# Hybrid token mixer and mixture-of-experts trunk on one core: an adaLN row's sum over the partitions placed in the middle of the following tile

## Chip, core and metric

The kernel runs on one core of a Trainium2 chip. The metric is device microseconds of one execution; three runs of the kernel before gave 3958.64, 3955.86 and 3944.15 us, the median is 3955.86 us. Profiles come from one execution each. PE is TensorE, DVE is VectorE, ACT is ScalarE, POOL is GpSimd, SP is SyncE; PEq, SPq and so on are the queues from which these engines take their instructions in order.

## What is computed

One layer on 4096 tokens of width 1024. A conditioning vector `c` gives six rows of 1024 numbers (shift, scale and gate for each of two sub-layers), which modulate a normalised `x`; the first sub-layer projects that into four head groups and mixes tokens, the second is a mixture of 64 experts.

```python
c_act = jax.nn.silu(c)
mod = c_act @ ada_w[l] + ada_b[l]                      # 1024 -> 6 x 1024
sh_m, sc_m, gt_m, sh_f, sc_f, gt_f = jnp.split(mod, 6, axis=-1)
h = modulate(rmsnorm(x, mix_norm_g[l]), sh_m, sc_m)
p = h @ w_in[l]                                        # split into the head groups
o_a, o_b, o_c, o_d = ...                               # delta rule, spatial gating, short conv, RWKV-7
x = x + gt_m[:, None, :] * (jnp.concatenate([o_a, o_b, o_c, o_d], -1) @ w_out[l])
h = modulate(rmsnorm(x, ffn_norm_g[l]), sh_f, sc_f)
x = x + gt_f[:, None, :] * hier_moe(h, ...)
return rmsnorm(x, final_norm_g)
```

The change concerns how four of the six rows of `mod` (numbers 2 to 5) are made. Rows 0 and 1 are needed for the first tile and are made before it.

## The kernel before

`run` goes through the stages `first`, `gdn`, `rwkv`, `outp`, `moe` and `final`. Only `first` is touched. It works on eight tiles (t = 0 to 7) of 512 tokens. For tile t, `first_tile` (line 930) has PE project the normalised and modulated tokens `h` with several slices of `w_in`: four matmul groups for the value half of the spatial gate and eight small columns (lines 944 to 958, the "sv" part), two groups for the other half (960 to 965, "su"), then after a reciprocal square root (966) and `norm()` (967) two groups for the low-rank inputs (974 to 981, "lx"). Tiles 0, 1 and 2 also do a short convolution (1002); tiles 3 to 7 do not. The spatial gating's own matmuls (1014) end the tile.

While a tile is projected, the input of the next is prepared. `h_rows` (255) loads its four blocks of 128 rows of `x` through the SP queue into the buffer ring with the tag `hx`, which has six buffers, and sums the squares on ACT. `h_norm` (270), called by `norm()` in the middle of `first_tile`, scales the rows on DVE. `h_make` (276) transposes them on PE (282), modulates on ACT, splits into a high and a low part on DVE (286, 288) and stores both to DRAM through the POOL queue (289, 290); its eight steps are woven between the matmuls of the second lx group (tiles 3 to 6) or of the convolution (tiles 0 to 2). The buffers of the x rows come free when the last transpose has read them, at the end of the tile.

The rows of `mod` ride along. A row is a sum over 1024 = 8 x 128 inputs: `ada_step` (199) loads one block of `ada_w`, 128 x 1024, through the SP queue into the same `hx` ring (208) and adds it, times the conditioning vector, to an accumulator on DVE (211, 213). The accumulators have the tag `adaa`, with two buffers. After eight steps `ada_row` (215) loads a row of `ada_b` through SP (219), sums the accumulator over the partitions with two fp32 matmuls against a column of ones (223, two instructions each on PE), adds the halves to the bias on DVE (224) and stores the row to DRAM through SP (227, 230), where stages much later read it. The 32 steps are dealt out five per tile (1129), so rows 2, 3, 4 and 5 end in tiles 1, 3, 4 and 6, the steps that end them being the third, first, fourth and second of their tile.

What sets the order: within `first` the order of PE's instructions is that of the program text (`manual_schedule(engines=PE)`, 1122). The order on the other engines and their queues is worked out by a planner from its own estimates of time, with program order as the priority; every engine then takes its instructions strictly in that order, each waiting for its inputs and for a free buffer. PE's order at a tile with a finished row is therefore: the row's four matmul instructions, then the tile's sv, su and lx parts.

When `first` is over its buffers are given to `gdn`, whose weights are loaded (351, tile `hraw`) into memory that the `hx` ring and others held.

Of the kernel before, what the change touches and what calls it, by code (L numbers as in the profile page):

```python
# [8 lines left out]
F32 = mybir.dt.float32  # L9
# [10 lines left out]
D = 1024  # L20
# [14 lines left out]
def tp(tc, name, bufs=1, **k):  # L35
    return tc.tile_pool(name=name, bufs=bufs, reuse_waits="tile", **k)
# [6 lines left out]
class Trunk:  # L43
# [168 lines left out]
            else:  # L212
                V.scalar_tensor_tensor(acc, w, self.cact[:, k:k + 1], acc, op0=ALU.mult, op1=ALU.add)

    def ada_row(self, pool, psum, j, ptag):

        nc, A = self.nc, self.A
        row = pool.tile([128, D], F32, name="adar", tag="adaa", bufs=2)
        nc.sync.dma_start(row[0:1], A["ada_b"][0:1, j * D:j * D + D])
        for n in range(2):  # L220
            s = slice(n * 512, n * 512 + 512)
            ps = psum.tile([128, 512], F32, name="adap", tag=ptag)
            nc.tensor.matmul(ps[0:1], self.one_c, self.ada_acc[:, s], start=True, stop=True)
            nc.vector.tensor_tensor(row[0:1, s], row[0:1, s], ps[0:1], op=ALU.add)
        if j == 3:

            nc.sync.dma_start(self.modd[j:j + 1].rearrange("o (k q) -> o q k", k=KT),
                              row[0:1].rearrange("o (q k) -> o q k", k=KT))
        else:
            nc.sync.dma_start(self.modd[j:j + 1], row[0:1])  # L230
# [859 lines left out]
    def first(self):  # L1090
        tc, A = self.tc, self.A
        with ExitStack() as c:
            pool_ = lambda n, b=1, **k: Pool(c.enter_context(tp(tc, n, b, **k)), n, b)
            wp, hp, pool, hw = pool_("f_w"), pool_("f_h", 18), pool_("f"), pool_("f_hw")
            psum = BufPsum(pool_("f_ps", space=PSUM), {"big": 6, "ada": 2})
            raw = lambda: hw.tile([128, D], F32, name="wraw", tag="hx", bufs=6)
            self.ada_begin(hw, psum, "ada")
            xs, ss = self.h_rows(hw, 0)
            self.h_norm(hw, xs, ss)
            self.f_sv = [wp.tile([128, KT, 264], F32R, name=f"sv{x}") for x in ("h", "l")]  # L1100
            self.f_su, self.f_x, self.f_c = (self.w_tiles(wp, n, nm) for n, nm in ((256, "su"), (256, "lx"), (768, "cv")))
            w = A["w_in"][0]
            self.h_setup(hw, hp, psum, "ada")
            raw2 = lambda: hp.tile([128, TB], F32R, name="wraw2", tag="hsl").bitcast(F32)
            self.w_load(self.f_sv, raw2, TB, w, 1288)
            self.w_load(self.f_sv, raw2, TB, w, 1024, 8, 256)
            h = [], []
            for _ in self.h_make(hw, hp, psum, "big", 0, xs, h):
                pass

            room = [("fu", 2), ("fco", 2), ("fu", 2), ("fco", 2), ("fx0", 1), ("fx1", 1), ("fy", 1), ("fhx", 1)]

            def raw3():
                n, b = room.pop(0)
                return pool.tile([128, TB], F32, name="wraw3", tag=n, bufs=b)
            self.w_load(self.f_su[0], raw3, TB, w, 1032)
            self.w_load(self.f_x[0], raw3, TB, w, 3080)
            self.first_setup(wp, pool, raw, psum, "ada")
            for g in (2, 1, 0):
                self.w_load(self.f_c[g], raw, D, w, 1544 + 256 * g)  # L1120
            n = -(-4 * KT // (self.NT - 1))
            with tc.manual_schedule(engines=PE):
                for t in range(self.NT):
                    norm, make, h1 = (lambda: None), iter(()), ([], [])
                    if t + 1 < self.NT:
                        xs, ss = self.h_rows(hw, t + 1)
                        norm = lambda xs=xs, ss=ss: self.h_norm(hw, xs, ss)
                        make = self.h_make(hw, hp, psum, "big", t + 1, xs, h1)
                    for i in range(n * t, min(n * t + n, 4 * KT)):
                        j, k = 2 + i // KT, i % KT  # L1130
                        self.ada_step(hw, j, k)
                        if k == KT - 1:
                            self.ada_row(hw, psum, j, "ada")
                    self.first_tile(pool, psum, t, h, norm, make)
                    if t == 1:
                        self.out_room(hw)
                    h = h1
# [927 lines left out]
```

## Time and profile before

| | |
|---|---|
| median of three runs | 3955.86 us |
| the profiled execution itself | 3957.31 us |
| its span in the trace | 3955.6 us |
| around the span | 1.7 us |
| PE busy | 3387.7 us (86% of the span) |
| DVE busy | 2533.8 us (64%) |
| ACT busy | 1730.6 us (44%) |
| granted PE clock, mean over the span | 0.919 |

Read it so: the span is what one execution lasts from its first to its last traced instruction. The trace tells for each instruction when it began, how long it took, and what ended the idle time ahead of it on its engine. The views by window give, for a stretch of time, the busy time of every engine, the share of full speed that PE's clock was granted (PEclk) and the mean busy share of the 16 DMA engines (DMA share). A PE wait matters if nothing behind it on PE could have run elsewhere; a wait of another engine matters only if PE ends up waiting for it.

### The profile page before, as it was taken

The page shows a single profiled execution, that of the slowest core. Times are in us where ns is not written, and L with a number is a line of the kernel's source. Part 1 is how long each engine was busy: PE and PEld are TensorE (multiplying, and loading weights), DVE is VectorE, ACT ScalarE, POOL GpSimd, SP SyncE. Part 2 cuts the span into 40 slices and gives each one's busy share as a digit, 9 for nine tenths or more (in the row PEclk, how much of TensorE's full clock was granted, in tenths as well). Part 3 has the DMA queues.
Part 4 walks back from the last instruction along what each step waited for, and adds up shares of the span by engine and source line. Part 5 has one row for each costly group of instructions (what it writes and reads, how often), then busy time and mean ns, then how long its engine had stood idle before and what let it go on. Part 6 is the DMA issues. An engine that isn't in the chain of part 4 may idle for free. (4 is left out here: it accounts for less than half of the span.)

```text
span 3955.6 us, 75069 instructions
## 1 busy us (share of the span) xinstructions
PE 3387.7 (86%) x28290; PEld 2874.6 (73%) x28290; DVE 2533.8 (64%) x6235; ACT 1730.6 (44%) x3236; POOL 1205.2 (30%) x1285
## 2 busy tenths in 40 slices
PE   6897878998988969999999799998589998998890
PEld 5686667888888957878888687786467776776770
DVE  6454557777777446776775366676675766567754
ACT  4233345556556134555553222222453544355543
POOL 1121222222222013434441011212454554355541
PEclk8998889899898979999999899999799999999995
DMA  8344552323223342333333544341897988789968
GB/s 288 119 172 169 187 166 73 98 81 81 79 78 109 110 136 74 102 91 88 85 96 115 157 172 155 128 144 65 268 319 205 282 281 275 213 258 327 306 178 345
DMA packets 462281, 659.78 MB, mean 167 GB/s; under 512 B 190895, under 2 KB 331463, under 8 KB 461710
## 3 DMA queue, kind: packets, MB, share of 16 engines
q1 hardware_dynamic: 393470, 465.98, 35.9%
q0 software_dynamic: 68240, 186.54, 16.5%
q8 instruction: 316, 5.18, 0.5%
q14 instruction: 255, 2.09, 0.2%
HBM read 520.00 MB, written 180.57 MB: 177 GB/s over the span
## 5 line engine op out<-in xcount | busy, mean ns | idle before, releaser
L1770 PE MATMUL mgu<-mgh,mxh 128*128 128x512 f32 x752 | 320.4, 426 | 76.8 <-PEq L1929 39.8
L1735 DVE TENSOR_TENSOR mgl<-mraw,mgh 128x1024 fp32r<-128x1024 f32 x256 | 302.8, 1225 | 66.8 <-ACT mgh L97 59.0
L1771 PE MATMUL mgu<-mgl,mxh 128*128 128x512 f32 x752 | 308.7, 410 | 0.0
L1772 PE MATMUL mgu<-mgh,mxl 128*128 128x512 f32 x752 | 308.4, 410 | 0.0
L97 ACT ACTIVATE mgh<-mraw 128x1024 fp32r<-128x1024 f32 x256 | 256.6, 1051 | 110.4 <-PEq L1929 82.7
L1811 POOL DMA_INDIRECT mxg<-h2d,ltg x156 | 198.8, 1274 | 184.9 <-DMA mxg<-h2d,ltg 62.5
L1770 PEld LDWEIGHTS mgu<-mgh,mxh 128*128 128x128 f32 x752 | 148.7, 198 | 131.7 <-issue 78.2
L1742 POOL TENSOR_TENSOR mdl<-mraw,mdh 128x1024 fp32r<-128x1024 f32 x64 | 168.7, 2636 | 85.5 <-issue 71.2
L1772 PEld LDWEIGHTS mgu<-mgh,mxl 128*128 128x128 f32 x752 | 148.8, 198 | 37.5 <-DVE mxl L1758 1.9
L1771 PEld LDWEIGHTS mgu<-mgl,mxh 128*128 128x128 f32 x752 | 149.4, 199 | 29.8
L83 ACT ACT_TABLE_LOAD x123 | 157.8, 1283 | 3.2 <-PEq L2051 0.8
L1801 PE MATMUL mdn<-mdh,mhh 128*128 128x512 f32 x376 | 155.3, 413 | 1.5 <-ACT mhh L97 0.8
L1802 PE MATMUL mdn<-mdl,mhh 128*128 128x512 f32 x376 | 148.6, 395 | 5.4 <-POOL mdl L1742 5.4
L1803 PE MATMUL mdn<-mdh,mhl 128*128 128x512 f32 x376 | 150.4, 400 | 3.2 <-DVE mhl L1788 2.8
L1399 POOL TENSOR_TENSOR gSd<-gSb,gcd 128x256 f32<-128x256 f32 x64 | 53.2, 831 | 308.3 <-DVE gSb L1410 307.0
L97 ACT ACTIVATE mhid<-mgu 128x256 f32<-128x256 f32 x94 | 35.4, 376 | 238.8 <-PE mgu L1772 238.8
L1778 DVE TENSOR_TENSOR mhid<-mhid,mgu 128x256 f32<-128x256 f32 x94 | 39.2, 417 | 156.6 <-ACT mhid L97 94.0
L1758 DVE TENSOR_TENSOR mxl<-mtp,mxh 128x512 fp32r<-128x512 f32 x188 | 120.8, 684 | 23.2 <-ACT mxh L97 23.1
L1647 PE MATMUL ops<-wo0h,ohi 128*128 128x512 f32 x256 | 106.7, 417 | 27.7 <-ACT ohi L97 27.5
L1806 POOL DMA_INDIRECT acc<-my,mpt x64 | 108.1, 1689 | 71.7 <-DVEq L1929 18.5
L97 ACT ACTIVATE mdh<-mraw 128x1024 fp32r<-128x1024 f32 x128 | 127.6, 1049 | 0.0
L1755 PE MATMUL mtp<-ident,mxg 128*128 128x128 f32 x752 | 99.6, 276 | 29.9 <-DMA mxg<-h2d,ltg 29.7
(555 smaller groups left out, 11439.2 us busy)
## 6 DMA issues: line engine op xcount, KB each, us to landing
mraw<-in_moe_w_gate_dram SPq DMA_DIRECT2D x128, 512.0 KB, 7.8
mraw<-in_moe_w_up_dram SPq DMA_DIRECT2D x128, 512.0 KB, 7.8
mraw<-in_moe_w_down_dram SPq DMA_DIRECT2D x128, 512.0 KB, 7.6
hhi<-hs_hi SPq DMA_DIRECT2D x168, 256.0 KB, 4.5
hlo<-hs_lo SPq DMA_DIRECT2D x168, 256.0 KB, 4.7
hx<-in_x_dram SPq DMA_DIRECT2D x32, 512.0 KB, 6.4
hs_hi<-hhi POOLq DMA_DIRECT2D x64, 256.0 KB, 7.0
hs_lo<-hlo POOLq DMA_DIRECT2D x64, 256.0 KB, 6.9
```

The lines of the kernel that those rows point to most:

```text
L83: ld = self.nc.scalar.preload_act_table_set(name)
L97: i = self.nc.scalar.activation(out, in_, func, bias=bias, scale=scale, **kw)
L1735: self.nc.vector.tensor_tensor(lo, raw, hi.bitcast(F32), op=ALU.subtract)
L1742: (nc.vector, nc.gpsimd)[f].tensor_tensor(lo, raw, hi.bitcast(F32), op=ALU.subtract)
L1758: nc.vector.tensor_tensor(xl[:, s, :], ps, xh[:, s, :].bitcast(F32), op=ALU.subtract)
L1770: nc.tensor.matmul(ps, xh[:, k, :], gh[:, k, :], start=(k == 0), stop=False)
L1771: nc.tensor.matmul(ps, xh[:, k, :], gl[:, k, :], start=False, stop=False)
L1772: nc.tensor.matmul(ps, xl[:, k, :], gh[:, k, :], start=False, stop=(k == KT - 1))
L1801: nc.tensor.matmul(ps, hh[:, f, :], dh[:, f, s], start=(f == 0), stop=False)
L1802: nc.tensor.matmul(ps, hh[:, f, :], dl[:, f, s], start=False, stop=False)
L1803: nc.tensor.matmul(ps, hl[:, f, :], dh[:, f, s], start=False, stop=(f == 1))
L1811: self.nc.gpsimd.indirect_dma_start(out=xg, out_offset=None, in_=self.h2d, in_offset=bass.IndirectOffsetOnAxis(ap=tg[:, 0:1], axis=0), bou ...
```

## The change

The finished accumulator is no longer reduced at once. `first` keeps a list, `todo`, of the rows that end in a tile, with their accumulators. In the next tile the list becomes `rows`, and a function `mid` takes the place of `norm`: it calls `norm()` and then `ada_row` for each entry. `first_tile` calls it where it called `norm()`, behind the su part and ahead of the lx part. `ada_row` is given the accumulator, since `self.ada_acc` may by then be the next row's. The tile that receives the row of `ada_b` moves from the `adaa` ring of two to the `hx` ring of six. So rows 2, 3, 4 and 5 are reduced in the middle of tiles 2, 4, 5 and 7.

```diff
-    def ada_row(self, pool, psum, j, ptag):
+    def ada_row(self, pool, psum, j, ptag, acc):
...
-        row = pool.tile([128, D], F32, name="adar", tag="adaa", bufs=2)
+        row = pool.tile([128, D], F32, name="adar", tag="hx", bufs=6)
         nc.sync.dma_start(row[0:1], A["ada_b"][0:1, j * D:j * D + D])
         for n in range(2):
             s = slice(n * 512, n * 512 + 512)
             ps = psum.tile([128, 512], F32, name="adap", tag=ptag)
-            nc.tensor.matmul(ps[0:1], self.one_c, self.ada_acc[:, s], start=True, stop=True)
+            nc.tensor.matmul(ps[0:1], self.one_c, acc[:, s], start=True, stop=True)
             nc.vector.tensor_tensor(row[0:1, s], row[0:1, s], ps[0:1], op=ALU.add)
...
             n = -(-4 * KT // (self.NT - 1))
+            todo = []
...
+
+                    rows, todo = todo, []
                     for i in range(n * t, min(n * t + n, 4 * KT)):
                         j, k = 2 + i // KT, i % KT
                         self.ada_step(hw, j, k)
                         if k == KT - 1:
-                            self.ada_row(hw, psum, j, "ada")
-                    self.first_tile(pool, psum, t, h, norm, make)
+                            todo.append((j, self.ada_acc))
+                    mid = lambda norm=norm, rows=rows: (norm(), [self.ada_row(hw, psum, j, "ada", x) for j, x in rows])
+                    self.first_tile(pool, psum, t, h, mid, make)
```

## Rows read from the trace of the kernel before

**Rows 1.** The page's first line:

```profile
span 3955.6 us, 75069 instructions
```

**Rows 2.** Who TensorE (PE) waited for, 62 to 556 us: total, times, longest:

```profile
PE adap L223 <- DVE adaa L213: 60.8, 4, 19.5
...
PE hps L282 <- DVE hx L274: 3.2, 4, 2.6
```

**Rows 3.** Windows between one tile's last matmul and the next tile's own first:

```profile
core 0: us, PE busy (x) PEld busy (x) DVE busy (x) ACT busy (x) POOL busy (x), PEclk, DMA share, GB/s
...
127.60:147.80 20.20, 3.52 (x5) 0.35 (x5) 8.55 (x12) 2.68 (x5) 4.17 (x8) 0.59 0.90 334
...
291.60:306.40 14.80, 3.45 (x4) 0.34 (x4) 5.02 (x9) 2.70 (x5) 3.61 (x7) 0.62 0.99 370
...
346.70:369.70 23.00, 3.49 (x5) 0.34 (x4) 11.79 (x19) 5.55 (x8) 6.08 (x11) 0.57 0.89 319
...
458.90:475.50 16.60, 3.45 (x4) 0.34 (x4) 8.25 (x14) 4.95 (x8) 3.88 (x8) 0.61 0.75 282
```

**Rows 4.** Windows of whole tiles, t = 1 to 7, same columns:

```profile
147.80:219.80 72.00, 72.00 (x402) 62.03 (x401) 29.10 (x76) 21.38 (x35) 10.12 (x19) 1.00 0.18 60
...
219.80:291.60 71.80, 71.75 (x402) 61.69 (x400) 36.74 (x86) 23.73 (x40) 15.71 (x28) 1.00 0.52 184
...
306.40:346.70 40.30, 40.30 (x257) 35.82 (x256) 22.50 (x58) 14.40 (x25) 4.89 (x8) 0.97 0.29 90
...
369.70:409.00 39.30, 39.30 (x257) 34.98 (x256) 18.80 (x55) 15.32 (x27) 8.62 (x15) 0.99 0.25 81
...
409.00:458.90 49.90, 45.27 (x260) 38.72 (x256) 31.17 (x76) 21.56 (x36) 14.12 (x26) 0.90 0.64 225
...
475.50:514.90 39.40, 39.40 (x258) 34.98 (x257) 18.52 (x54) 13.37 (x23) 8.54 (x16) 0.99 0.20 64
...
514.90:554.20 39.30, 37.93 (x226) 33.03 (x224) 17.20 (x50) 13.18 (x20) 8.46 (x16) 0.96 0.65 225
```

**Rows 5.** Timeline at the head of tile 4: start us, us, engine, line, instruction:

```profile
345.73 18.98 SPq L208 DMA_DIRECT2D adaw<-in_ada_w_dram  x5
...
364.88 1.28 DVE L213 SCALAR_TENSOR_TENSOR adaa<-adaw,cact,adaa 128x1024 f32<-128x1024 f32 x1
...
366.21 3.57 PE L223 MATMUL adap<-adaa,one_c 128*1 128x512 f32 x4 [19.51 <-DVE adaa L213]
```

**Rows 6.** The SyncE queue's own waits, 0 to 560 us:

```profile
SPq L264 <- PE hps L282: 144.8, 6, 42.8
```

**Rows 7.** Windows for the clock: row matmuls, su stage, first stage of tiles 4 and 5:

```profile
366.21:369.71 3.50, 3.50 (x4) 0.34 (x5) 1.22 (x2) 0.00 (x0) 0.54 (x1) 0.50 0.72 224
...
424.50:435.50 11.00, 11.00 (x51) 9.12 (x50) 6.21 (x12) 0.38 (x1) 0.54 (x1) 1.00 0.60 190
...
369.70:381.70 12.00, 12.00 (x97) 11.99 (x97) 4.47 (x13) 4.27 (x9) 3.95 (x6) 0.97 0.47 149
...
409.00:424.50 15.50, 14.12 (x100) 13.42 (x97) 8.73 (x21) 6.59 (x11) 4.79 (x9) 0.89 1.00 387
```

**Rows 8.** Timeline of tile 5, ACT:

```profile
435.79 0.63 ACT L97 ACTIVATE fxh<-fx 128x512 fp32r<-128x512 f32 x1 [10.66 <-DMA oT<-fm]
```

**Rows 9.** Groups by shape, 60 to 556 us; and the page's DMA issues:

```profile
L224 DVE TENSOR_TENSOR adar<-adar,adap 1x512 f32<-1x512 f32 x8 | 5.4, 673 | 6.8 <-PE adap L223 6.8
...
hx<-in_x_dram SPq DMA_DIRECT2D x32, 512.0 KB, 6.4
```

**Rows 10.** Start of the next stage: SyncE and ACT timeline, and landing of line 351:

```profile
512.87 14.80 SPq L351 DMA_DIRECT2D hraw<-in_w_in_dram  x4
...
DMA to landing us min/median/max: 12.0/14.5/17.0
...
552.93 1.90 ACT L97 ACTIVATE gd1h<-hraw 128x2048 fp32r<-128x2048 f32 x1
```

**Rows 11.** Window of the two stages that follow, same columns as rows 3:

```profile
554.20:2240.00 1685.80, 1520.47 (x18998) 1356.10 (x18998) 1138.99 (x3490) 828.07 (x1796) 447.54 (x602) 0.93 0.34 95
```

## The prediction, made before the changed kernel was run

> **What bounds the kernel now.** I read the page first: one core, one program of several stages, so a change in `first` has to be judged in its 554 us and not by shares of the span [rows 1]. Second, who PE waited for inside `first`: a single entry matters, the row matmuls of line 223, which waited four times for the accumulator, 60.8 us in all; the next, the transposes waiting for the normalised x, is 3.2 us [rows 2]. Third, the windows between tiles: they place those waits. Four of the seven gaps between one tile's last matmul and the next one's sv part are 20.2, 14.8, 23.0 and 16.6 us long, 74.6 us together, at the heads of tiles 1, 3, 4 and 6, and PE is busy only 3.5 us in each, with the four row instructions [rows 3]. Inside the tiles PE is full: 72.00 of 72.0 us, 40.30 of 40.3, 39.30 of 39.3 [rows 4]. So `first` is bound by PE's program order, with these four holes in it.
>
> Fourth, the head of tile 4 in order of time, to see why the accumulator is late. The x rows of the next tile and the blocks of `ada_w` share one ring; its loads wait on the SP queue for the transposes that end the tile (144.8 us of such waits in `first`) [rows 6]. Only then do five blocks go out, over 19.0 us; DVE starts the last sum that the row needs at 364.9 us and PE goes on at 366.2 us [rows 5]. The loads cannot start much sooner; but the sv and su matmuls behind the row on PE need nothing of it.
>
> **The change, part by part.**
>
> *Removed.* The four heads: 74.6 us [rows 3], of which 60.8 us is waiting [rows 2] and 4 x 3.5 = 14.0 us is matmuls.
>
> *Added on PE.* The same four instructions per row, now behind the su part. At the head of tile 4 they take 3.50 us at a granted clock of 0.50, that is 1.2 GHz, after an idle PE; the su part runs at 1.00, that is 2.4 GHz [rows 7]. No row shows them at full clock, so the price lies between half of 3.50, 1.75 us, and 3.50 us. I take 1.75, since in the middle PE has been busy for 12.0 + 11.0 us [rows 7]. The accumulator has been finished for half a tile, so nothing waits there. In tiles 2 and 7 this is path: 3.5 us. In tiles 4 and 5 I expect it to stand in front of a wait for the normalised x like that of tile 5, 3.2 us [rows 2], and to cost nothing more; without that cover it costs another 3.5 us.
>
> *Given back by tiles that lose their head.* While PE stands, DMA, DVE and ACT catch up on the last tile's stores and splits. Tile 5, which had no row, shows a tile without this pause: 49.9 us against 39.3 for tile 4 [rows 4]. Its first part takes 15.5 us instead of 12.0, DMA share 1.00 [rows 7]; ACT then stands 10.7 us on a store of the spatial gating left from tile 4 [rows 8], which makes the x rows late, and PE's clock sags (0.90 over the tile [rows 4]).
> - Tile 1 follows and has a convolution. Tile 2, the same without a row, lasts 71.8 us against 72.0 [rows 4]: 0 lost; a loss would have to outlast the convolution, which stands ahead of the transposes.
> - Tile 3 follows a convolution tile, whose low-rank stores are made early: 0 to 10.6 us. I take 1, by its neighbour tile 2.
> - Tile 4 becomes like tile 5, with the same five blocks to load: I take the whole 49.9 - 39.3 = 10.6 us; at least 15.5 - 12.0 = 3.5.
> - Tile 6 loads only two blocks: 3.5 to 10.6; I take 5, nearer to tile 7, which loads none and lasts 39.3 us with no head [rows 4].
>
> *Other queues.* SP: the load of `ada_b` and the store of the row move past the following tile's x and `ada_w` loads; behind the store stand the x loads of the tile after, which wait for the end of the tile in any case [rows 6]. DVE: two additions of 0.67 us per row [rows 9] now stand near `h_norm`, and with them a wait for the `ada_b` load, which needs a buffer of the `hx` ring; behind it on DVE stand the splits that PE needs. Hidden by the 1.75 us of matmuls and the lx part; if not, some microseconds in tiles 4 and 5, inside the bound above. The accumulators have two buffers, so the first step of row 5, in tile 4, must wait on DVE for row 3 in the middle of tile 4; its next step belongs to tile 5. POOL's queue is passed by nothing.
>
> *Hand-over to `gdn`.* The first weight loads are issued at 512.9 us and land within 17.0 us of their issues, and ACT uses them from 552.9 [rows 10]. They reuse the ring's memory, and row 5 now sits there until the middle of tile 7, about 514.9 + 15.5 + 11.0 + 1.8 = 543 us on the old clock [rows 4, 7], 30 us behind the old first issue. Slack is 552.9 - 512.9 - 17.0 = 23 us: 0 to about 24 us late. I take 3, as only one of the loads has to meet the row's buffer.
>
> *Sum.* 74.6 - 3.5 (tiles 2, 7) - 1 - 10.6 - 5 - 3 = 51.5 us gained. The profiled execution took 3957.3 us, 1.4 us more than the median of the runs: 3955.9 - 51.5 = 3904.4, say **3905 us**.
>
> **Rivals.**
> 1. *The ring is the bound, and the change takes one more of its buffers.* Then every tile from 3 on without a pause lasts as long as tile 5: 49.9 us in place of 14.8 + 40.3, 23.0 + 39.3 and 16.6 + 39.4 us [rows 3, 4], which saves 5.2 + 12.4 + 6.1 = 23.7 us; tile 1 saves 20.2; the matmuls cost 4 x 1.75 = 7.0; the late hand-over, another 12. That is 24.9 us gained, **3931 us**. For: the ring's 144.8 us of queue waits [rows 6]. Against: tile 6 has little to load. The Trainium skill, Perfetto Trace Analysis, section "Optimization Strategy", says that equal bubbles in a stretch can mean that a tile lacks buffers to be allocated; by that reading the change would shift the wait and not end it. The trace agrees that loads wait for buffers, and does not show that PE has to.
> 2. *DMA is the bound.* In the heads the DMA engines are busy 0.75 to 0.99 of the time; all four together 20.2 x 0.90 + 14.8 x 0.99 + 23.0 x 0.89 + 16.6 x 0.75 = 65.8 us [rows 3]. If all of it came back, 8.8 us would be left, **3947 us**. Against: under tile 4 the share is 0.25 and under tile 6 0.20, so 39.3 x 0.75 = 29 and 39.4 x 0.80 = 32 us are free there for 20.5 and 12.5 [rows 4].
> 3. *Slower: the planner's order in the next two stages.* It orders DVE, ACT and the queues by estimated times that run on from `first`; moved estimates can order `gdn` and `rwkv` differently. There PE idles 1685.8 - 1520.5 = 165.3 us [rows 11]. If that grew by half, 83 us, the whole would take 3905 + 83 = **3988 us**; it is slower from a growth of 51.5 us, a third, on. For: DVE is busy 68% there and little slack stands between the chains. Against: PE's order is written by hand and no operation changes.
> 4. *It does nothing*, because the row's matmuls still meet an unfinished sum in the middle: 3956 us. Half a tile, 12.0 + 11.0 us [rows 7], speaks against.
>
> **How the numbers follow.** A difference of 0.5%, 20 us, is about what a measurement of this kernel can tell from none. Forecast 0.62; rival 1 0.18; rival 2 0.07; rival 3 0.09; rival 4 0.04. Rival 1 stays under 3936 us in 0.15 of its 0.18. Faster: 0.62 + 0.15 = 0.77; same: 0.03 + 0.07 + 0.04 = 0.14; slower: 0.09. The forecast's own range: at best nothing is lost but 7.0 us of matmuls and 3.5 us each in tiles 4 and 6, 60.6 us, 3895 us; with tile 3 and tile 6 at their ends (9.6 + 5.6) and matmuls of 3.50 us (3.5 more), 32.8 us, 3923 us. The range reaches up over rival 1 and 7 us more of a late hand-over, 3938 us, and a little below the best sum, 3890 us; it leaves out rivals 2, 3 and 4, 0.20.
>
> **What would show it.** Right: no PE wait on line 213 is left; the row matmuls stand at 1.75 us behind the su part in tiles 2, 4, 5, 7; tiles 4 and 5 last some 50 us, tile 6 some 44, tile 3 some 41; PE ends `first` near 554.2 - 54.5 = 500 us (the sum without the hand-over); `gdn` and `rwkv` keep 1686 us. Wrong: tiles of over 55 us, with the transposes waiting for x (rivals 1, 2), a first `gdn` matmul more than 12 us behind the end of `first`, or a different length of the two stages (rival 3).

## The result, and the profile after

The median of four runs is **3895.74 us** (3885.82 to 3900.61), against 3957.25 us for four runs of the kernel before: a ratio of 0.9848, 95% interval 0.9824 to 0.9873. That is 61.5 us less, where 51.5 us less was forecast; the range and the sign held. The profiled execution took 3895.57 us, 0.2 us from the median, so it can stand for the runs. Its page begins:

```profile
span 3893.8 us, 75055 instructions
...
PE 3381.8 (87%) x28290; PEld 2872.8 (74%) x28290; DVE 2531.7 (65%) x6235; ACT 1728.5 (44%) x3236; POOL 1207.8 (31%) x1285
```

The span is 61.8 us shorter [rows 1], PE's busy time hardly changes: what went is idle time. Next what PE waited for, now from 62 to 500 us, since `first` ends earlier:

```profile
PE pbig L1014 <- ACT hf L97: 5.6, 1, 5.6
PE hps L282 <- DVE hx L274: 4.0, 6, 2.7
...
PE hps L282 <- ACT hf L97: 1.1, 1, 1.1
```

The 60.8 us at line 223 are gone [rows 2]. The wait of the transposes for x (line 282) grew by 0.8 us only, and one new wait of 5.6 us has come, at the spatial gating's matmuls (line 1014). Then the windows, with the columns of [rows 3]: tiles 1 to 7, which now follow each other without a gap; then row 2's matmuls in tile 2; a stretch of tile 3; the first parts of tiles 4 and 5; `gdn` and `rwkv`; and the rest of the program.

```profile
127.40:199.10 71.70, 71.70 (x404) 61.70 (x400) 35.55 (x86) 23.50 (x39) 14.48 (x26) 1.00 0.44 155
199.10:273.20 74.10, 74.03 (x407) 61.94 (x404) 38.15 (x90) 24.04 (x40) 15.62 (x28) 1.00 0.50 177
273.20:319.30 46.10, 42.78 (x261) 36.96 (x257) 27.31 (x68) 17.49 (x31) 8.65 (x16) 0.93 0.61 212
319.30:371.20 51.90, 43.86 (x263) 36.30 (x261) 30.17 (x73) 20.80 (x36) 14.74 (x27) 0.97 0.65 230
371.20:413.80 42.60, 41.71 (x262) 34.99 (x260) 31.40 (x75) 20.98 (x36) 13.34 (x25) 1.00 0.59 205
413.80:454.30 40.50, 39.71 (x258) 34.82 (x256) 25.20 (x67) 18.00 (x30) 12.10 (x23) 1.00 0.51 189
454.30:495.80 41.50, 40.06 (x228) 33.23 (x228) 18.69 (x53) 13.30 (x20) 8.56 (x16) 0.96 0.60 200
222.17:223.97 1.80, 1.80 (x5) 0.25 (x4) 1.64 (x9) 0.00 (x0) 0.00 (x0) 1.00 0.60 239
305.40:311.00 5.60, 4.88 (x14) 3.51 (x15) 5.60 (x14) 1.67 (x3) 0.00 (x0) 0.55 0.00 0
...
319.30:331.30 12.00, 11.33 (x93) 11.12 (x92) 7.38 (x17) 6.12 (x11) 4.86 (x10) 1.00 0.96 360
...
371.20:383.30 12.10, 11.21 (x89) 10.74 (x88) 8.21 (x20) 6.07 (x11) 3.76 (x7) 1.00 0.97 360
...
502.00:2182.90 1680.90, 1524.11 (x19008) 1360.71 (x19009) 1132.90 (x3486) 821.10 (x1791) 451.53 (x602) 0.93 0.33 95
2182.90:3893.80 1710.90, 1410.61 (x6752) 1133.18 (x6750) 1107.63 (x2074) 709.93 (x1128) 646.56 (x481) 0.92 0.72 232
```

PE ends `first` at 495.8 us where it ended at 554.2 [rows 4]: 58.4 us of the 61.8 are won there. The first `gdn` matmul follows 6.2 us later in this trace and 6.4 us later in that of before, and from it to the first load of the third stage (line 235) pass 1680.9 us after and 1680.6 before. The last stages are 3.5 us shorter; in the experiments below, which leave those stages as they are, that part lasts 1714 to 1735 us in one execution or another, so these 3.5 us can't be put down to the change. The DMA share under tiles 3, 4 and 6 rose from 0.29, 0.25 and 0.20 [rows 4] to 0.61, 0.65 and 0.51: the transfers that filled the heads [rows 3] now run under the tiles.

### The profile page after: what moved, and what is told of

Its sections match the earlier page's. It is cut to its first block, busy times and chain, and to the rows that moved or that the text cites. A ratio compares the mean times of both kernels' runs of the same rounds, so it can differ in the third digit from the quotient of the medians.

```text
span 3893.8 us, 75055 instructions
## 1 busy us (share of the span) xinstructions
PE 3381.8 (87%) x28290; PEld 2872.8 (74%) x28290; DVE 2531.7 (65%) x6235; ACT 1728.5 (44%) x3236; POOL 1207.8 (31%) x1285
```

## The experiments

All are edits of the kernel after, but for the third, which is one of the kernel before. The columns are: median of the runs; ratio to the kernel before in the same job, with its 95% interval; PE's end of `first`, the time from the last matmul of tile 2 to the last of tile 5, and the length of `gdn` and `rwkv` up to line 235's first load, all three from the profiled execution. There is one such execution for each kernel, and it can lie well off the median: that of the plain store took 3884.71 us, that of the next head 3917.37. The control does the same as the kernel after but for four matmuls of one column, and its `first` ends 2.6 us earlier; differences of that size in these columns show nothing.

| kernel | median us | ratio | `first` ends | tiles 3 to 5 | `gdn`+`rwkv` |
|---|---|---|---|---|---|
| before | 3957.25 | 1 | 554.2 | 167.3 | 1680.6 |
| after | 3895.74 | 0.9848 [0.9824, 0.9873] | 495.8 | 140.6 | 1680.9 |
| wait put back | 3955.38 | 1.0011 [0.9994, 1.0028] | 550.1 | 164.6 | 1678.9 |
| its control | 3896.49 | 0.9854 [0.9833, 0.9875] | 493.2 | 138.2 | 1681.0 |
| before, buffer alone | 3954.01 | 0.9998 [0.9984, 1.0013] | 552.1 | 165.4 | 1680.8 |
| own tile | 3893.37 | 0.9840 [0.9820, 0.9861] | 487.5 | 135.8 | 1675.8 |
| next head | 3903.80 | 0.9866 [0.9840, 0.9892] | 501.0 | 149.4 | 1673.6 |
| other ring | 3900.97 | 0.9870 [0.9854, 0.9887] | 503.9 | 151.6 | 1674.2 |
| plain store | 3900.83 | 0.9872 [0.9855, 0.9889] | 494.4 | 141.0 | 1666.7 |
| blocks dealt anew | 3880.31 | 0.9815 [0.9796, 0.9835] | 482.4 | 126.3 | 1670.5 |
| ten blocks a tile | 3880.67 | 0.9815 [0.9794, 0.9836] | 482.8 | 125.9 | 1668.7 |

### Is it the wait? The wait put back, and its control

At the head of the tile where a row ends, a matmul of one column reads the finished accumulator; nobody reads its result, and the row itself stays in the middle of the next tile. The control issues the same matmul on a constant in place of the accumulator (`self.wsT[:, 0, 0:1]`).

```diff
                             todo.append((j, self.ada_acc))
+                            ps = psum.tile([128, 512], F32, name="adaq", tag="ada")
+                            self.nc.tensor.matmul(ps[0:1, 0:1], self.one_c, self.ada_acc[:, 0:1], start=True, stop=True)
```

> The changed kernel, and at the head of tiles 1, 3, 4 and 6 one matmul of a single column that reads the finished accumulator, its result unused: the wait alone is put back, not the row's matmuls, not the row's buffer, not the additions. Theory (the gain is the wait that stood at the head of PE's order): PE waits for line 213 again four times, 55 to 65 us in all, and the whole goes back to 3944 to 3956 us, short of the kernel before by the matmuls at half speed, about 7 us. Rival (the gain is the planner's new order of the other engines, or the row's other ring): it stays at 3896 to 3905 us.

> The control to the wait put back: the same four single-column matmuls at the heads of tiles 1, 3, 4 and 6 of the changed kernel, but they read a constant weight tile and not the accumulator. Theory (it was the wait): some tenths of a us on PE, the whole at 3896 us, give or take 8. Rival (a matmul of its own at the head breaks the stream of PE, its clock or the planner's order): 3910 us or more.

Who PE waited for with the wait put back (line 1138 is the added matmul), and then with the control, over all of `first`:

```profile
PE adaq L1138 <- DVE adaa L213: 60.3, 4, 19.4
```

```profile
PE pbig L1014 <- ACT hf L97: 5.5, 1, 5.5
PE hps L282 <- DVE hx L274: 3.5, 7, 1.8
```

The four waits are back with 60.3 us against 60.8 [rows 2], and so is the whole time: 3955.38 us, no difference from before within the interval. The same number of instructions without the wait keeps the gain. So the gain hangs on the wait at the head of PE's queue. What else the change brought is small: with the wait put back PE still ends `first` 4.1 us earlier than before, with the row matmuls no longer at the heads, and the medians don't tell this apart.

### The other half of the change by itself

The kernel before, with only the tile of `ada_b`'s row moved to the `hx` ring:

```diff
-        row = pool.tile([128, D], F32, name="adar", tag="adaa", bufs=2)
+        row = pool.tile([128, D], F32, name="adar", tag="hx", bufs=6)
```

> The kernel before with the other half of the change alone: the row's buffer comes from the hx ring, the matmuls stay at the head of the row's own tile. Theory: the four waits for line 213 stay near 61 us and the whole at 3955 us, give or take 10; row 3 is stored in a pause, where its slow store delays x loads that PE does not yet need. Rival (the gain comes from the ring or from the planner's new order): 3900 to 3930 us. If the taken buffer costs loads, the waits grow beyond 61 us: 3965 us or more.

Its list of PE's waits:

```profile
PE adap L223 <- DVE adaa L213: 60.0, 4, 19.5
```

3954.01 us, a ratio of 0.9998 with an interval of 0.15% to either side: the buffer neither gains nor costs where PE stands at the heads anyway.

### Does the place matter? The row's own tile, and the next tile's head

The first variant reduces the row in the middle of the tile in which it ends, a whole tile earlier than the change; the second at the head of the next tile, half a tile earlier than the change.

```diff
-                    rows, todo = todo, []
+                    rows = []
...
-                            todo.append((j, self.ada_acc))
+                            rows.append((j, self.ada_acc))
```

```diff
-                    rows, todo = todo, []
+                    for j, x in todo:
+                        self.ada_row(hw, psum, j, "ada", x)
+                    todo = []
...
-                    mid = lambda norm=norm, rows=rows: (norm(), [self.ada_row(hw, psum, j, "ada", x) for j, x in rows])
+                    mid = norm
```

> The rows are reduced in the middle of the tile in which they end, and not of the next. In the kernel before, the sums were ready 16.7, 11.4, 19.5 and 13.2 us behind the end of the previous tile; the middle comes 22.7 us or more behind it. Theory: no wait at the row matmuls, the whole at 3896 us, give or take 6. Rival: with PE running, DMA brings the blocks later (tile 5 before had its last sum 24 us behind its start), so that PE waits some us in tiles 1 and 4, rows with the third and fourth block: 3900 to 3915 us.

> The row is reduced at the head of the tile after the one in which it ends, ahead of the sv part, and not in its middle: the sum has been finished for half a tile or more, so by the theory (only the wait for the sum matters, not where in the tile the matmuls stand) PE does not wait at line 223, the four instructions take 1.8 us, and the whole is 3896 us, give or take 8. Rival: at the head the additions on DVE and the ada_b load meet the burst of loads and stores, and the rows' buffers are taken when the ring is fullest; then the tiles with a row, 2, 4, 5 and 7, grow by some us each: 3905 to 3915 us.

The largest entry of PE's waits in `first` with the row in its own tile:

```profile
PE hps L282 <- DVE hx L274: 4.6, 10, 1.1
```

No wait for the accumulator: half a tile is enough, and the time is that of the change (3893.37 us, intervals that overlap), though `first` ends 8.3 us earlier in its trace. With the row at the next head there is no such wait either, but tile 4 lasts 56.7 us. PE's wait in that tile, and then the SyncE queue (start, duration, line, transfer):

```profile
PE hps L282 <- DVE hx L274: 12.0, 3, 11.6
```

```profile
324.02 0.63 SPq L227 DMA_DIRECT2D modd<-adar  x1
327.53 16.49 SPq L208 DMA_DIRECT2D adaw<-in_ada_w_dram  x4
347.28 26.65 SPq L264 DMA_DIRECT2D hx<-in_x_dram  x4
```

Row 3's store (line 227) now stands in the queue ahead of four of the tile's five blocks; they go out from 327.5 to 344.0 us, the next x loads from 347.3 us on, and the transposes wait 11.6 us for the normalised x. So the place does matter, by what is queued behind the row's store on SP and not by PE's order. (The median's 8 us above the kernel after lie within the two intervals; the 56.7 us in tile 4 are in the trace.)

### What is still lost in tile 4? The ring, or the store

After the change tile 4 lasts 51.9 us. In order of time, SyncE, ACT and PE of the kernel after in that tile; the line at 341.5 us and the last three, from the hand-over, are read further down:

```profile
348.80 0.34 SPq L264 DMA_DIRECT2D hx<-in_x_dram  x1
349.55 0.63 SPq L227 DMA_DIRECT2D modd<-adar  x1
360.04 4.22 SPq L264 DMA_DIRECT2D hx<-in_x_dram  x3
...
341.51 0.63 ACT L97 ACTIVATE fxh<-fx 128x512 fp32r<-128x512 f32 x1 [8.98 <-DMA oT<-fm]
...
356.20 1.06 ACT L97 ACTIVATE hjk<-hx 128x1024 bf16<-128x1024 f32 x1 [6.21 <-DMA hx<-in_x_dram]
...
365.98 1.06 ACT L97 ACTIVATE hjk<-hx 128x1024 bf16<-128x1024 f32 x1 [4.84 <-DMA hx<-in_x_dram]
...
367.85 3.39 PE L1014 MATMUL pbig<-wsT,fvf 128*64 128x128 f32 x32 [5.60 <-ACT hf L97]
...
483.49 0.24 SPq L230 DMA_DIRECT2D modd<-adar  x1
483.83 5.29 SPq L351 DMA_DIRECT2D hraw<-in_w_in_dram  x4
...
494.52 1.90 ACT L97 ACTIVATE gd1h<-hraw 128x2048 fp32r<-128x2048 f32 x1
```

Row 3 is stored at 349.6 us in permuted order, 1024 single numbers. One x load was issued before it, three only 10.5 us behind it. These rows are for a later tile, but ACT's sums of squares (`hjk`) for the first two of them stand ahead of steps of `hf`, which the current transposes need, in ACT's queue; ACT waits 6.21 and 4.84 us for x, and PE waits 5.60 us for `hf`. SyncE's own waits of the kernel after show that the x loads waited for the landing of the row's store (`modd<-adar`), and the wait at the hand-over:

```profile
SPq L230 <- DVE frt L175: 56.7, 1, 56.7
...
SPq L264 <- DMA modd<-adar: 12.8, 3, 9.8
```

One theory is that the buffer counts: the row sits in the `hx` ring and the x loads wait until its store has landed. The rival is the store itself, or what the tile has to load. The first test takes the row out of the ring: rows 3 to 5 go in two halves through two small buffers of a ring (`fco`) that the tiles without a convolution leave idle.

```diff
-    def ada_row(self, pool, psum, j, ptag, acc):
+    def ada_row(self, pool, psum, j, ptag, acc, other=None):
...
+        if other is not None:
+            for n in range(2):
+                row = other.tile([128, 512], F32, name="adar", tag="fco", bufs=2)
...
-                    mid = lambda norm=norm, rows=rows: (norm(), [self.ada_row(hw, psum, j, "ada", x) for j, x in rows])
+                    mid = lambda norm=norm, rows=rows: (norm(), [self.ada_row(hw, psum, j, "ada", x, pool if t > 2 else None) for j, x in rows])
```

> Rows 3, 4 and 5 get two half buffers of the ring fco, which lies idle from tile 3 on, in place of one of the six hx buffers; all else as in the changed kernel (3895.7 us). Theory R: in tile 4 PE's waits of 5.6 and 1.1 us for ACT (the transposes' modulation) come from an x load that waited for row 3's buffer, so that ACT's sum of squares, ahead of the modulation in its queue, waited too. Then tile 4 falls from 51.9 to about 45 us and the whole to about 3889 us. Rival S: that x load is late by the ring itself, whatever the row occupies; then tile 4 stays at 51 to 52 us and the whole at 3896 us.

SyncE and ACT of this kernel in tile 4 (line numbers are 14 higher behind the edit):

```profile
349.88 0.63 SPq L227 DMA_DIRECT2D modd<-adar  x1
350.61 0.55 SPq L278 DMA_DIRECT2D hx<-in_x_dram  x1
351.29 2.39 SPq L227 DMA_DIRECT2D modd<-adar  x1
...
364.79 1.06 ACT L97 ACTIVATE hjk<-hx 128x1024 bf16<-128x1024 f32 x1 [13.05 <-DMA hx<-in_x_dram]
```

Freeing the buffer alone doesn't help. The x load needs no buffer of the row's any more and is issued at 350.6 us, between the two halves of the permuted store; yet ACT gets its data only at 364.8 us, hardly sooner than the 366.0 us of the kernel after, 14.2 us after the issue, where the median landing of these loads before was 6.4 us [rows 9]. Tile 4 lasts 57.2 us and tile 5 48.4, worse than after. The second test stores row 3 in one piece; a copy from DRAM to DRAM, which stands behind the last tile in the program, permutes it.

```diff
-            nc.sync.dma_start(self.modd[j:j + 1].rearrange("o (k q) -> o q k", k=KT),
-                              row[0:1].rearrange("o (q k) -> o q k", k=KT))
+            self.row3 = self.dram.tile([1, D], F32, name="row3")
+            nc.sync.dma_start(self.row3, row[0:1])
...
+            self.nc.sync.dma_start(self.modd[3:4].rearrange("o (k q) -> o q k", k=KT),
+                                   self.row3.rearrange("o (q k) -> o q k", k=KT))
```

> Row 3 stays in the hx ring but is stored to DRAM in one piece; the permuting copy, 1024 single numbers, follows from DRAM to DRAM behind the last tile. Theory R, with the slow permuted store (x loads waited up to 9.8 us for it) as what holds the buffer: tile 4 falls from 51.9 to about 45 to 46 us, the whole to about 3890 us. If the buffer's mere use by the row is enough, tile 4 stays near 52 us and the whole near 3896 us.

The windows of tiles 4 and 5, and SyncE in tile 4 with its wait for the row's store (`row<-adar`):

```profile
318.80:362.80 44.00, 42.43 (x263) 34.93 (x261) 28.82 (x70) 19.86 (x35) 14.23 (x25) 1.00 0.68 211
362.80:414.00 51.20, 45.92 (x261) 37.52 (x261) 33.51 (x81) 22.45 (x38) 15.32 (x29) 0.93 0.65 234
```

```profile
352.63 0.33 SPq L264 DMA_DIRECT2D hx<-in_x_dram  x1
353.01 0.60 SPq L1142 DMA_DIRECT2D modd<-row  x1
...
SPq L264 <- DMA row<-adar: 3.0, 1, 3.0
```

The planner, which orders SyncE's queue, did not leave the copy (line 1142) behind the last tile: it goes out at 353.0 us, in tile 4 as well. What this kernel changes is what stands ahead of the second x load: it waits 3.0 us for the row's buffer in place of 9.8 and goes out at 352.6 us, ahead of the permuting copy and not behind a permuted store. Tile 4 drops from 51.9 to 44.0 us, a little further than expected. So the permuted store does hold tile 4 up, by the buffer that it keeps in the kernel after and by delaying a load near it with the other ring. But tile 5 rises from 42.6 to 51.2 us, tiles 3 to 5 take 141.0 us against 140.6, and the whole is not faster. Whether the copy has a part in tile 5's rise was not tried: a kernel with five blocks in each of these tiles and no permuted transfer is missing.

### What do tiles 3 to 5 have in common? Their five blocks

Tiles 0 to 2 have a convolution that stands ahead of the transposes, and cover their loads. The last experiments give them eight blocks each and later tiles two; rows 2 to 5 then end in tiles 0, 1, 2 and 6, and are reduced in the middle of tiles 1, 2, 3 and 7. A second dealing is `[8, 10, 10, 1, 1, 1, 1, 0]`.

```diff
-            n = -(-4 * KT // (self.NT - 1))
+            deal = [8, 8, 8, 2, 2, 2, 2, 0]
...
-                    for i in range(n * t, min(n * t + n, 4 * KT)):
+                    for i in range(sum(deal[:t]), sum(deal[:t + 1])):
```

> The changed kernel with the 32 blocks of ada_w dealt 8, 8, 8, 2, 2, 2, 2, 0 over the tiles and not 5, 5, 5, 5, 5, 5, 2, 0; the rows are then reduced in the middle of tiles 1, 2, 3 and 7. Theory D: what tiles 3, 4 and 5 lose (46.1, 51.9 and 42.6 us against 40.5 for tile 6 with two blocks) comes from their five blocks, which pass through two free buffers behind the x loads. Then tiles 3 to 5 fall to 40 to 44 us each (3 with a row's 1.8), the convolution tiles stay at 72 to 74 us, and the whole is 12 to 16 us below the changed kernel, near 3882 us. Rival L: it comes from the last tile's stores (low-rank parts, spatial gating), which a tile without a convolution pushes into the next; then tile 3 changes little, tiles 4 and 5 keep 45 us and more, and the whole stays at 3890 to 3896 us.

> The same with 8, 10, 10, 1, 1, 1, 1, 0. Theory D: tiles 3 to 6 at 39.5 to 41 us, about 5 us less in all than with two blocks per tile, if ten blocks still fit into a convolution tile (ten at some 4.7 us each, 47 us, ahead of transposes that begin 62 us into the tile): near 3878 us. If they do not fit, PE waits for x or for the sums in tiles 1 and 2 and these grow beyond 75 us: 3885 us or more.

Windows of tiles 3 to 6 with the first dealing, and the two largest entries of PE's waits in its `first`:

```profile
274.20:315.50 41.30, 41.30 (x263) 34.91 (x261) 25.75 (x68) 17.40 (x32) 8.77 (x16) 1.00 0.56 198
315.50:357.30 41.80, 40.50 (x259) 34.74 (x257) 24.64 (x65) 19.93 (x34) 13.72 (x26) 1.00 0.55 196
357.30:400.50 43.20, 41.71 (x256) 36.41 (x256) 26.36 (x69) 20.74 (x35) 13.18 (x25) 0.96 0.57 207
400.50:442.50 42.00, 40.41 (x257) 34.89 (x257) 26.34 (x70) 18.67 (x31) 13.27 (x25) 1.00 0.52 194
```

```profile
PE pbig L950 <- DVE hlo L288: 4.3, 7, 0.7
PE hps L282 <- DVE hx L274: 0.9, 3, 0.3
```

Tiles 3 to 5 take 126.3 us in place of 140.6, no single wait is over 0.7 us, and tiles 1 and 2, with eight blocks and a row each, take 73.8 us each, as much as tile 2 after with five and a row. `first` ends 13.4 us earlier. With 3880.31 us (3879.84 to 3881.86) this version stands 15.4 us below the change and 71.2 us below the kernel before of the same job; the two ratios, 0.9815 and 0.9848, have intervals that overlap a little, and the 13.4 us of the trace bear the gain out. Dealing still fewer blocks to the late tiles brings nothing more (3880.67 us).

The new dealing moves more than blocks: row 3 with its permuted store is now reduced in tile 2, and tiles 4 and 5 have no row. For tile 3 the blocks are the cause that is left: it has no row in the kernel after, gets one here, and still falls from 46.1 to 41.3 us. Tile 5 of the kernel before, with five blocks and no row, took 49.9 us [rows 4]. How the 9.5 us won in tiles 4 and 5 divide between the blocks, the two rows' matmuls and row 3's store is not shown, nor whether a block costs by the ring's buffers, SyncE's queue or the DMA engines.

One difference is left open. Six of the kernels run `gdn` and `rwkv` 5 to 14 us faster than before though no operation there was touched; none runs them over 0.5 us longer. What in those stages makes it was not tried, and with one profiled execution of each kernel it may be the execution and not the kernel.

## Why the prediction was right, step by step

**Removed: right.** The four heads were idle time set by program order: the put-back wait and its control show that this wait carries the gain.

**Row matmuls: right, at the lower bound.** 1.80 us at a granted clock of 1.00 in tile 2, against 1.75 forecast and 3.50 at a clock of 0.50 [rows 7]. The groups by shape of the kernel after show the same over all four rows (total, mean ns of one, idle before):

```profile
L223 PE MATMUL adap<-adaa,one_c 128*1 128x512 f32 x16 | 7.5, 591 | 0.0
...
L224 DVE TENSOR_TENSOR adar<-adar,adap 1x512 f32<-1x512 f32 x8 | 5.3, 672 | 6.5 <-PE adap L223 6.5
```

DVE's additions wait 6.5 us for PE in all, as before [rows 9], and PE never waits for the accumulator. Rival 4 is out, by more than the half tile that was forecast: row 3's last addition ended at 284.7 us and its matmuls began at 342.9. The cover in tiles 4 and 5 was wrong: the transposes there wait 0.7 us and not at all for the normalised x, where 3.2 us were to hide the row. In tile 4 the wait of 5.60 us at line 1014 came behind the row's matmuls instead and could hide them; in tile 5 no such wait came.

**Tiles without their head: the sum right, the parts not.** Against the plan of 41.3, 49.9 and 49.9 us, tiles 3, 4 and 5 took 46.1, 51.9 and 42.6: 140.6 against 141.1. Errors of +4.8, +2.0 and -7.3 us cancel.
- Tile 3 was mis-sized: 1 us by its neighbour with a convolution, where 5.8 came. The transposes waited 2.67 us for x, and from 305.4 to 311.0 us the granted clock was 0.55, near 1.2 GHz, behind that wait. The normalisation was late because ACT squares two x rows of the tile after ahead of it, and their loads went out behind the five blocks (lines below). The bound of 0 to 10.6 held; the low choice in it did not.
- Tile 4 had the right size by another mechanism, which is luck. Its first part took 12.0 us at a DMA share of 0.96, not 15.5. ACT did stand 8.98 us, up to 341.5 us, on the store left from tile 3's gating, as it did in tile 5 before [rows 8]; but the squares that the transposes needed were done by then, and these waited only 0.7 us for x. Row 3's permuted store did the harm. I had counted the store's place in SP's queue as harmless, since the x loads behind it wait for the end of the tile in any case. They do not all: the first x load was issued ahead of the store, at 348.8 us, three behind it at 360.0 us.
- Tile 5 was taken as unchanged at 49.9 us. Its first part took 12.1 us at a DMA share of 0.97, not 15.5 at 1.00 [rows 7]. PE had stood some 8 us in tile 4, and the plain store shows the reverse, a short tile 4 with a tile 5 of 51.2 us; but a stall in one tile does not always spare the next: the other ring has 57.2 and 48.4 us. Why tile 5 lost so little is open.
- Tile 6 was mis-sized the other way: 5 us forecast, 40.5 - 39.4 = 1.1 us measured, below the lower bound of 3.5. With two blocks there was almost nothing to give back.

SyncE and ACT in tile 3 of the kernel after:

```profile
272.72 17.95 SPq L208 DMA_DIRECT2D adaw<-in_ada_w_dram  x5
292.46 3.25 SPq L264 DMA_DIRECT2D hx<-in_x_dram  x2
...
297.10 1.06 ACT L97 ACTIVATE hjk<-hx 128x1024 bf16<-128x1024 f32 x1 [11.57 <-DMA hx<-in_x_dram]
```

**Hand-over: the order right, the cost 0 instead of 3 us.** All four weight loads did move behind row 5's store: SyncE waited 56.7 us to issue it, up to 483.5 us, and the loads followed up to 489.1 us. ACT used the first at 494.5 us, without a wait for it and still before PE's end of `first`: it had landed at most 10.7 us after the first issue, where 17.0 was allowed for [rows 10]. The first `gdn` matmul waits there, in both traces alike, for the stored `h` to come back (6.4 us before, 6.2 after), not for a late weight load.

**The sum.** Of the 10.3 us that the gain in span (61.8) exceeds the forecast (51.5), 3.9 are in `first`, nearly all in tile 6, 3 in the hand-over, and 3.5 in the last stages, where executions differ by more.

**Rivals.** Rival 1 gave 49.9 us to tiles 3, 4 and 6 and a late hand-over; they took 46.1, 51.9 and 40.5, and the hand-over cost nothing. It was right in part in tile 4, where x loads did wait for the row's buffer, up to 9.8 us; but with the row in the other ring tile 4 took 57.2 us, so the buffer is not the bound. The Trainium skill, Perfetto Trace Analysis, section "Optimization Strategy", says that equal bubbles can mean too few buffers for the next tile. For the bubbles removed here the runs say otherwise: the waits ended with the order changed and one buffer fewer free in the `hx` ring. Rival 2 is out: most of the heads' 65.8 us of DMA work fits under the tiles, at shares of 0.51 to 0.65. Rival 3 is out: `gdn` and `rwkv` kept their length to 0.3 us.

## What to carry to other kernels

An engine that takes its instructions in order pays for one late operand with everything behind it. Where independent work stands behind such an instruction, move the instruction by the time that its operand is late, here half a tile, and count its stores and loads in the queues that they now pass. When the wait is gone, look at how the loads are dealt: moving three of five out of each tile that couldn't cover them, and row 3's store with them, won 14 us over three tiles, and eight per tile cost next to nothing where a longer tile could cover them.

## What the runs showed of the hardware

- A store of 1024 single numbers delays its neighbours: it was 10.5 us until the x loads that needed its buffer went out, and with a load issued between its two halves 14.2 us until that load's data were used, where the median landing before was 6.4 us [rows 9]. Which part of the path it holds the runs don't tell.
- A short wait can cost more than itself: 2.67 us of standing were followed by 5.6 us at a granted clock of 0.55, nearly all of it at the lower level of 1.2 GHz.
- The DMA engines were 0.97 busy over the first 12.1 us of tile 5 while PE was busy for 11.2 of them; the first part of tile 5 before, at a share of 1.00, took 15.5 us [rows 7]. The share alone does not tell the two apart.
